# Seven-product pairs of a hybrid decoder step: sums formed in PSUM banks, and equal halves in the mixer

## The chip, the cores and the metric

The kernel runs on one core of one Trainium2 chip. The core has TensorE (PE; PEld is its loading of weights), VectorE (DVE), ScalarE (ACT), GpSimd (POOL) and SyncE (SP), which issues most DMAs. TensorE writes its products to PSUM, which has eight banks of 512 numbers for each of 128 partitions; the kernel holds four of them under the tag "acc" and four under the tag "ps". The metric is the device time of one execution in microseconds (us); lower is better.

## The reference

One inference step of one decoder layer, for 512 prompt tokens with 16 meta tokens ahead of them, and for 8 sequences of 4 new tokens: in all 560 columns of tokens, of which 544 (the meta tokens left out) go on after attention. The model has width 1024 and 2816 hidden units.

```python
def swiglu(x, w_gate, w_up, w_down):
    return (jax.nn.silu(x @ w_gate) * (x @ w_up)) @ w_down

h = x + 0.5 * rms_norm(swiglu(rms_norm(x, ffn1_pre_g), ...), ffn1_post_g)
u = rms_norm(h, mix_pre_g)
proj = u @ w_in      # q, k, v, rank and r of the GLA branch; q, k, v of attention; gate_a, gate_b
...
o_a = rms_norm(o_a, gla_norm_g) * jax.nn.silu(r_a)
m = jax.nn.sigmoid(gate_a) * (o_a @ w_o_gla) + jax.nn.sigmoid(gate_b) * (o_b @ w_o_sb)
h = h + rms_norm(m @ w_out, mix_post_g)
y = h + 0.5 * rms_norm(swiglu(rms_norm(h, ffn2_pre_g), ...), ffn2_post_g)
```

All values are float32.

## The kernel before

Activations are held turned: 128 features in the partitions, tokens along the columns. Each operand of a large product is split in two parts, a high part hi (a cast to the type fp32r) and a low part lo (what is left), and a product of two is three matmuls: hi with hi, hi with lo, lo with hi. A weight block is loaded by DMA into one of three buffers "raw"; ScalarE casts it into one of three buffers "hi", VectorE subtracts into one of three buffers "lo". Buffers of a name are used in turn.

The stages are: first feed-forward part (gate and up products, then the down product), w_in products with GLA and attention, the mixer (gates r, a and b, and the products o and p with w_o_gla and w_o_sb), the product with w_out, the second feed-forward part. The order on TensorE, VectorE, ScalarE and GpSimd is written out by hand: a product is a generator that yields after every few matmuls, each yield is one step, and `later(n, f)` and `when(n, f)` put a piece of work in the n-th step from now or from the start of a stage. Within a step work stands in the order in which it was asked for, and work of `later` ahead of work of `when`.

**Pairs of seven products.** Where two blocks of weights and two halves of the tokens meet, four quarter products are formed from seven instead of eight (a scheme of Strassen and Winograd). This is done for 16 pairs in each of the two feed-forward parts (`seven`, L1221, gate and up of one tile f), for 10 pairs in the mixer (`seven_steps`, L1016, through `r_pair`, L2320, and `gate_pair`, L2352), and for the down products (`pair`, L1371, which the change leaves as it is). A pair has 84 matmuls in 14 steps of six. They come in seven phases of 12, each with one bank as its target; the table at L1262 and L1042 lists bank, activation, weights and their quarter:

- a gets its first product; d the product of s1; b that of s2; c that of s3;
- a gets a second product and is then the result c11; d gets s4; c gets the product with t4.

The weights of a pair are cast as four groups: b1 (used by a and d), t (by b and c), b2 (by a and d), t4 (by c). `weights_at` (L1008) puts the cast of b1 six steps ahead of the pair, so in step 8 of the pair before, that of t two steps ahead, b2 with the start, and t4 in step 4. ScalarE copies the first products of a and d to SBUF (e1, e5), and five additions on VectorE do the rest: u2 = e1 + b, v = e5 + c, c22 = u2 + v, c12 = u2 + d, c21 = u2 + c. All pairs use the four banks "acc".

**Room.** SBUF tiles of the names "room" lie in an arena whose places come from a table (`PLACES`, L52).

**Plain products** in the mixer (`tile_steps`, L691) take the 544 columns as halves of 280 (`HW`) and 264 (`W1`); pairs take them as halves of 272 (`QW`). In the first feed-forward part a half has 280 columns, in the second 272.

Of the kernel before, what the change touches and what calls it, by code (L numbers as in the profile page):

```python
# [18 lines left out]
KD = D // P  # L19
# [33 lines left out]
0c060018121e242a7094908082848668766a5066565e5c787c5452724e7a5836221c884c8c6c3064484a6e60613a2e8a3e446236923c465a3036  # L53
281674404260917e91588e124e328c341e726c307e4a4c188a486e3e24647a882c3c38360c06625a6a42749244402a3a2e0c00605e5c1e201254
147c16220664465283006268826980660b50560660680a69866467808400620b660a0c2661066460676686186300606266671004650662646766
86286100646066671a10620660878663660c1c00621d8786640e2506662486871c60910064688786241a690666688687820a6800246564697662
6806666991008264690078680607082491770776681c069186424e3e343a74546e7266323c00368c4468767c2840781e6c820c0238708c762a2e
26927c8a040660622a2c4816246527702e1262186071152c622a2b2d6415712c1262632a622a2b2d642c71626306180c1e62714b71246a003254
883e64604b38020434308a6058763c786222122a482e4c4a8e2c7b84668c687e7f406056464f3d333579036b366e747044426c7215015939318b
7782893f055514157a804e5a7e825c2483284e655e92647c508d3a521e148c822667648466616764656766422c7016604668746c6e647244206a  # L60
0a6612088a6c1804343c8c780688916a761a720f026e22320e1c103057565584641486544000760c676a6c8a7248082e604c1a3e582a910e2c66
301c856e001257421002685655542040164675150c8a146a0a300e121e188c782a2c007074107620060421863442736c6e728988846475668e0c
17343e12324c4a42460b7476486a3c1c3004436e20080972621a3736876660860a436c8417686e8e6a642c1488568c430408063c906394708417
6664606c6e78728e8a68846a86606e17708468646a6c7894728e668a0c866e606c176478686a848e728a66706e6c866072177084026836646a6c
8e00786686948a6e401c6620721a1e178a646030948e106c0c6a0e181c2068708486366e786a4072102a221e20170094667038840e1a6e8e0c1c
60724068641c8a1e1a186c220260206e8e59540e2a0c84721e302e68100066606c94641e3840202200706694308e8464606e4740721002682e0e
6c6630002a6884548c880c1456648e6e701660946c586e0c040e463c144754621206329074442e087674582c0a6c160c40102e2c006611466e43
705658544472340862403010322a1200024406343090916e0a436d0610160c72620840909066466c726c625670540a58406e084672020e540a6e
44163c4000100c064614404372561213020410703c3d423e000e4c6e161246483c060444420b1048704c0a023e494072006e480e14166e424412
463c560a2a7460309461704c8c8d2e904a4862766660346c6d670e88303276406c8c6663629500102c623e8876947254586667000e0a01006667  # L70
00105466403e88560d0c7273000c068a508e86202264366a1e7c7880268492524e34603a141a7e487a68734246824a733c3e58901b1717722e38
6e174c2840245a17175c7074442a5e5d1876668c54509212583e903c12151556622c88526c1b484a464215687f7b7e7a151b683a4e601b6a845c
1b18678d8053932d3078156577556381891c2282516d57648a5e1272384c2e1e828e906e868418403e36582416749432426a340c00605a5c484a
30683c44463a0c4e62702a56882c121e922022066416547f00607a7e7b80660b768c0662640a650c6c677e7800640e66060a600f06620e67660c
7a1000641166670e0419066218676610801800641966671a0c1906621c181d660a1b0064241a251c18630666266227241a65001c286429261067
06244e664f280e5000261d1c064e62520624292800501c4f00264e080928062524020308006c14862c486672504c8e4e1268926052880208047a
64304a2e3c82600a5884220c0280566a622410460e1e360842000a060418200302060e10030211060c0d0504020c110304020e1005030c181e30
24363d3440243a3e243865268202906c626e70
# [56 lines left out]
def hybrid_step(  # L135
# [555 lines left out]
    def tile_steps(act, w1, order=range(KD)):  # L691

        wid = (HW, w1)
        hi, lo = st.parts.pop(0)
        acc = {h: ps("acc") for h in range(2)}
        for k in order:
            a = {h: act.get(k, h, wid[h]) for h in range(2)}
            for h in range(2):
                T.matmul(acc[h][:, : wid[h]], hi[k], a[h][0], start=(k == order[0]), stop=False)  # L699
                T.matmul(acc[h][:, : wid[h]], hi[k], a[h][1], start=False, stop=False)  # L700
# [315 lines left out]
    def seven_steps(f, act, qw, outs):  # L1016
# [6 lines left out]
        def add(name, x, y):  # L1023
            o[name] = take(HW)
            tt(o[name][:, :qw], o[x][:, :qw], y[:, :qw], ALU.add)
            give(o.pop(x))

# [4 lines left out]
        def made(name, x, y, last=None):  # L1032
            tt(outs[name], o[x][:, :qw], y, ALU.add)
            if last:
                give(o.pop(last))
# [58 lines left out]
    def other_tiles(old, gain, rs, nw, wid, hid, pairs, plan, late, sums_at, begun):  # L1094
# [126 lines left out]
        def seven(f):  # L1221
            a11, a12, a22 = ([ub.t[k0 + k, h] for k in range(4)] for h, k0 in ((0, 0), (0, 4), (1, 4)))
            s1, s2, s3, s4 = ([sums[j, k] for k in range(4)] for j in range(4))
            a, d, b, c = (ps("acc") for _ in range(4))
            o = {}

            def add(name, x, y):
                o[name] = take(HW)
                tt(o[name][:, :QW], o[x][:, :QW], y[:, :QW], ALU.add)
# [5 lines left out]
            def u2_():  # L1235
                add("u2", "e1", b)
                give(o["e1"])

            def v_():
                add("v", "e5", c)  # L1240
                give(o["e5"])

            def c22():
                o["up"], o["sl"] = take(NT), take(NT)
                tt(o["up"][:, QS[1]], o["u2"][:, :QW], o["v"][:, :QW], ALU.add)
                give(o["v"])

            def c21():
                tt(o["sl"][:, QS[1]], o["u2"][:, :QW], c[:, :QW], ALU.add)
                give(o["u2"])  # L1250
# [11 lines left out]
            for x, act, key, k0, first in ((a, a11, "b1", 0, True), (d, s1, "b1", 4, True), (b, s2, "t", 0, True), (c, s3, "t", 4, True),  # L1262
                                           (a, a12, "b2", 4, False), (d, s4, "b2", 0, False), (c, a22, "t4", 0, False)):
# [8 lines left out]
        waiting = []  # L1272
# [1001 lines left out]
    def split(dst, k, src, kept):  # L2274
# [3 lines left out]
        for h in range(2):  # L2278
            c = slice(h * HW, h * HW + W2[h])
# [19 lines left out]
    def gate_r(n):  # L2299

        o = oa_back(n)
        acc = yield from tile_steps(um, W1)
        sg = take(NW)

        def sig():
            for h in range(2):
                S.activation(sg[:, h * HW : h * HW + W2[h]], acc[h][:, : W2[h]], AF.Sigmoid)

        def by():
            for h in range(2):  # L2310
                c = slice(h * HW, h * HW + W2[h])
                tt(sg[:, c], acc[h][:, : W2[h]], sg[:, c], ALU.mult)
# [7 lines left out]
    def r_pair(n):  # L2320
# [12 lines left out]
        def first():  # L2333
            t[0] = take(NW)
            outs.update(c11=lambda a: S.copy(t[0][:, q0], a), c21=t[0][:, q1])
# [16 lines left out]
    def gate_pair(what, n):  # L2352
# [3 lines left out]
        outs = {"c11": lambda a: S.activation(t0[:, q0], a, AF.Sigmoid), "c12": t1[:, q0], "c22": t1[:, q1], "c21": t0[:, q1]}  # L2356
        later(15, lambda: S.activation(t1, t1, AF.Sigmoid))
        later(16, lambda: S.activation(t0[:, q1], t0[:, q1], AF.Sigmoid))
# [38 lines left out]
    def out_a(n):  # L2397
        acc = yield from tile_steps(oas, W1, (0, 1, 2, 7, 3, 4, 6, 5) if n == 0 else range(KD))
        m1.append(take(NW))

        def out():
            for h in range(2):
                S.copy(m1[n][:, h * HW : h * HW + W2[h]], acc[h][:, : W2[h]])
# [28 lines left out]
    with tc.manual_schedule(engines={E.PE, E.DVE, E.Activation, E.Pool}):  # L2432
# [31 lines left out]
        def product_b(n):  # L2464
            acc = yield from tile_steps(obs, W1)
            mixed(n, acc)

        def chain():
            mains = {"r": gate_r, "o": out_a, "p": product_b}
            for kind, what, t in MIXER:  # L2470
# [3 lines left out]
                if (what, t) == ("b", 6):  # L2474
                    later(1, lambda: give(*kept_sums, *(t for p in um.full.values() for t in p)))

# [107 lines left out]
        def mixed(n, acc):  # L2584
            t = sgb[n]

            def by():
                for h in range(2):
                    c = slice(h * HW, h * HW + W2[h])
# [160 lines left out]
```

## Time and profile before

| | |
|---|---|
| time, median of 3 runs | 1492.96 us (1492.42 to 1494.59) |
| profiled execution | span 1491.2 us from its first to its last instruction; its time with what lies around it is not listed |
| granted clock of TensorE | 0.999 of full speed |
| pairs, first part | 93.4 to 266 us |
| pairs, mixer | 832 to 1044 us |
| pairs, second part | 1179.5 to 1348 us |
| DMA | 182 MB, 122 GB/s on average |

The matmuls of a pair stand at L1266 to L1268 and L1046 to L1048, plain products of the mixer at L699, L700 and L702. The additions on VectorE are written through a helper, so all of them stand at L166 and are told apart by their tiles. A row of groups gives line, engine, operation, output and inputs, shape and count, then busy time, the mean of one in ns, and the idle time of the engine just before them with what ended it. Matmuls overlap: one lasts 290 ns from its start to its end, and the next starts some 128 ns after it.

### The profile page before, as it was taken

Reading aid. Unit: us, or ns where it says so; the run is one execution under the profiler, and the core shown is the slowest. Engines: PE = TensorE matmul, PEld = TensorE weight load, DVE = VectorE, ACT = ScalarE, POOL = GpSimd, SP = SyncE. Lnnn points to the kernel's source line nnn. Section 1 sums busy time; section 2 is a strip of 40 time slices with the busy share of each in tenths; the row PEclk is TensorE's granted clock in tenths of the full one; section 3 lists DMA queues with packets and bytes.
Section 4 is the critical chain, followed back from the end, with each engine's and each line's share of the span. In section 5 each row is a group of like instructions: output and inputs, shape, how many; then the busy total and the mean of one; then the engine's idle time right before and its main releaser. Section 6 shows DMA issues by size and latency. Waiting matters only on the chain.

```text
span 1491.2 us, 29865 instructions
## 1 busy us (share of the span) xinstructions
PE 1482.6 (99%) x11909; PEld 1435.2 (96%) x11909; DVE 1106.0 (74%) x1945; ACT 783.1 (53%) x1453; POOL 68.4 (5%) x145
## 2 busy tenths in 40 slices
PE   9999999999999999999999999999999999999998
PEld 8999999999999899999998999999999999999998
DVE  5888888855677866877887845777567898888544
ACT  7455454533555656566666543634564455455333
POOL 2000000000000011112111000000000000000000
PEclk9999999999999999999999999999999999999999
DMA  8133333324665584336555866344531333333253
GB/s 253 50 92 100 100 96 92 97 79 123 172 153 138 148 151 100 86 95 161 125 112 160 228 162 200 96 110 140 155 111 52 100 100 100 99 107 92 79 152 115
DMA packets 277230, 181.97 MB, mean 122 GB/s; under 512 B 10429, under 2 KB 255363, under 8 KB 277091
## 3 DMA queue, kind: packets, MB, share of 16 engines
q1 hardware_dynamic: 276786, 180.00, 44.7%
q8 instruction: 93, 1.52, 0.4%
q14 instruction: 47, 0.38, 0.1%
q0 software_dynamic: 288, 0.07, 0.0%
q10 hardware_dynamic: 16, 0.00, 0.0%
HBM read 155.06 MB, written 24.97 MB: 121 GB/s over the span
## 4 chain that ended last, share of the span: by engine, by line
PE 96%; DVE 2%; ACT 1%; DMA 1%; issue 0%; DVEq 0%; ACTq 0%
PE acc L1266 8%; PE acc L1267 8%; PE acc L1268 8%; PE acc L699 7%; PE acc L700 7%; PE acc L702 7%; PE acc L712 6%; PE acc L715 6%; PE acc L713 6%; PE acc L1046 2%; PE acc L1047 2%; PE acc L1048 2%; PE acc L1209 2%; PE acc L1206 2%; PE acc L1207 2%; PE ps L2041 1%
## 5 line engine op out<-in xcount | busy, mean ns | idle before, releaser
L166 DVE TENSOR_TENSOR room<-room,room 128x544 f32<-128x544 f32 (+18 forms) x457 | 285.6, 648 | 72.3 <-ACT room L779 16.7
L166 DVE TENSOR_TENSOR lo<-raw,hi 128x1024 fp32r<-128x1024 f32 (+1 forms) x207 | 248.1, 1199 | 105.5 <-ACT hi L678 66.7
L1266 PE MATMUL acc<-room,hi 128*128 128x280 f32 (+1 forms) x896 | 260.0, 290 | 0.0
L1268 PE MATMUL acc<-room,lo 128*128 128x280 f32 (+1 forms) x896 | 259.6, 290 | 0.0
L1267 PE MATMUL acc<-room,hi 128*128 128x280 f32 (+1 forms) x896 | 259.4, 289 | 0.0
L699 PE MATMUL acc<-room,hi 128*128 128x280 f32 x832 | 241.1, 307 | 0.2 <-DVE room L169 0.2
L700 PE MATMUL acc<-room,hi 128*128 128x280 f32 x832 | 225.0, 289 | 0.0
L977 ACT CAST hi<-raw 128x1024 fp32r<-128x1024 f32 x100 | 104.8, 1052 | 146.2 <-PE acc L1267 48.6
L702 PE MATMUL acc<-room,lo 128*128 128x280 f32 x832 | 173.1, 289 | 0.0
L1267 PEld LDWEIGHTS acc<-room,hi 128*128 128x128 f32 x896 | 168.9, 188 | 0.0
L1266 PEld LDWEIGHTS acc<-room,hi 128*128 128x128 f32 x896 | 168.8, 188 | 0.0
L1268 PEld LDWEIGHTS acc<-room,lo 128*128 128x128 f32 x896 | 168.6, 188 | 0.0
L699 PEld LDWEIGHTS acc<-room,hi 128*128 128x128 f32 x832 | 156.8, 188 | 10.1 <-issue 8.1
L700 PEld LDWEIGHTS acc<-room,hi 128*128 128x128 f32 x832 | 157.2, 189 | 1.2
L678 ACT CAST hi<-raw 128x1024 fp32r<-128x1024 f32 (+1 forms) x107 | 108.2, 1013 | 75.2 <-issue 21.5
L702 PEld LDWEIGHTS acc<-room,lo 128*128 128x128 f32 x832 | 130.3, 189 | 0.0
L977 ACT CAST hi<-room 128x1024 fp32r<-128x1024 f32 x92 | 76.9, 836 | 87.3 <-PE acc L1267 58.5
L166 DVE TENSOR_TENSOR lo<-room,hi 128x1024 fp32r<-128x1024 f32 x92 | 87.9, 955 | 43.4 <-ACT hi L977 43.0
L712 PE MATMUL acc<-room,hi 128*128 128x280 f32 (+2 forms) x388 | 110.8, 295 | 0.0
L713 PE MATMUL acc<-room,hi 128*128 128x280 f32 (+2 forms) x388 | 108.9, 290 | 0.0
L166 DVE TENSOR_TENSOR room<-room,acc 128x272 f32<-128x272 f32 (+1 forms) x180 | 76.2, 437 | 43.8 <-PE acc L1048 20.9
L712 PE MATMUL acc<-room,room 128*128 128x280 f32 (+3 forms) x364 | 107.4, 295 | 0.0
(397 smaller groups left out, 3437.2 us busy)
## 6 DMA issues: line engine op xcount, KB each, us to landing
raw<-in_w_in_dram SPq DMA_DIRECT2D x43, 512.0 KB, 7.2
raw<-in_ffn_w_gate_dram SPq DMA_DIRECT2D x64, 256.0 KB, 3.1
raw<-in_ffn_w_up_dram SPq DMA_DIRECT2D x64, 256.0 KB, 3.4
raw<-in_ffn_w_down_dram SPq DMA_DIRECT2D x36, 448.0 KB, 3.9
raw<-in_w_in_dram SPq DMA_DIRECT2D x40, 256.0 KB, 4.7
out_dram<-room SPq DMA_DIRECT2D x36, 256.0 KB, 3.7
room<-in_cache_k_dram SPq DMA_DIRECT2D x32, 256.0 KB, 5.7
room<-in_cache_v_dram SPq DMA_DIRECT2D x32, 256.0 KB, 4.7
```

The source lines that it names most:

```text
L166: (eng or V).tensor_tensor(out=out, in0=a, in1=b, op=op)
L678: S.copy(h_, src)
L699: T.matmul(acc[h][:, : wid[h]], hi[k], a[h][0], start=(k == order[0]), stop=False)
L700: T.matmul(acc[h][:, : wid[h]], hi[k], a[h][1], start=False, stop=False)
L702: T.matmul(acc[h][:, : wid[h]], lo[k], a[h][0], start=False, stop=(k == order[-1]))
L712: T.matmul(acc[h][:nw, : wid[h]], wh, a[h][0], start=(k == 0), stop=False)
L713: T.matmul(acc[h][:nw, : wid[h]], wh, a[h][1], start=False, stop=False)
L715: T.matmul(acc[h][:nw, : wid[h]], wl, a[h][0], start=False, stop=(k == kt - 1))
L977: S.copy(hi[:, :kt], src)
L1266: T.matmul(x[:, :QW], hi, act[k][0], start=(first and k == 0), stop=False, skip_group_check=True)
L1267: T.matmul(x[:, :QW], hi, act[k][1], start=False, stop=False, skip_group_check=True)
L1268: T.matmul(x[:, :QW], lo, act[k][0], start=False, stop=(k == 3), skip_group_check=True)
```

## The change

The pairs of `seven` and `seven_steps` keep their seven products and change how these are added. Bank b no longer starts from zero: ScalarE copies the finished first product of a into bank b, and b's matmuls add to it, so that b ends as u2. Then ScalarE copies b into bank c, and c's first product adds to that (u3 = u2 + product of s3); after the second product of c the bank holds c21. VectorE is left with c22 = u3 + e5 and c12 = u2 + d, and ScalarE copies e5, u2 and u3 to SBUF. The second product of a moves ahead of the first of c. c21 goes straight from bank c through ScalarE's function (Silu, Sigmoid, or a copy).

In `seven` the pairs use the banks "acc" and "ps" in turn; ahead of the second pair of each part, which is the first on "ps", one matmul each is written to b and c with start set. In the mixer the halves of plain products become 272 and 272. `PLACES` has new numbers for the changed order of tiles.

```diff
-    def tile_steps(act, w1, order=range(KD)):
-        wid = (HW, w1)
+    def tile_steps(act, w1, order=range(KD), w0=HW):
+        wid = (w0, w1)
...
         # seven_steps (mixer)
-        for n, g in ((3, lambda: copied("e1", a)), (5, lambda: copied("e5", d)), (7, lambda: add("u2", "e1", b)),
-                     (9, lambda: add("v", "e5", c)), (10, lambda: made("c22", "u2", o["v"][:, :qw], "v")),
-                     (11, lambda: outs["c11"](a[:, :qw])), (13, lambda: made("c12", "u2", d[:, :qw])),
-                     (15, lambda: made("c21", "u2", c[:, :qw], "u2"))):
+        def seeded(x, y):
+            S.copy(x[:, :qw], y[:, :qw])
+        for n, g in ((2, lambda: seeded(b, a)), (4, lambda: copied("e5", d)), (6, lambda: seeded(c, b)), (6, lambda: copied("u2", b)),
+                     (10, lambda: copied("u3", c)), (11, lambda: outs["c11"](a[:, :qw])), (11, c22),
+                     (12, lambda: made("c12", "u2", d)), (14, lambda: outs["c21"](c[:, :qw]))):
             later(n, g)
-        for x, act_, key, k0, first in ((a, a11, "b1", 0, True), (d, s1, "b1", 4, True), (b, s2, "t", 0, True), (c, s3, "t", 4, True),
-                                        (a, a12, "b2", 4, False), (d, s4, "b2", 0, False), (c, a22, "t4", 0, False)):
+        for x, act_, key, k0, first in ((a, a11, "b1", 0, True), (d, s1, "b1", 4, True), (b, s2, "t", 0, False), (a, a12, "b2", 4, False),
+                                        (c, s3, "t", 4, False), (d, s4, "b2", 0, False), (c, a22, "t4", 0, False)):
...
         # seven (feed-forward parts); its table of phases changes in the same way
-            a, d, b, c = (ps("acc") for _ in range(4))
+            tag = turns[len(turns_done) % 2]
+            turns_done.append(f)
+            a, d, b, c = (ps(tag) for _ in range(4))
-            for n, g in ((3, lambda: copied("e1", a)), (5, lambda: copied("e5", d)), (7, u2_), (9, v_), (10, c22),
-                         (11, lambda: S.activation(o["sl"][:, QS[0]], a[:, :QW], AF.Silu)),
-                         (13, lambda: tt(o["up"][:, QS[0]], o["u2"][:, :QW], d[:, :QW], ALU.add)), (15, c21),
-                         (16, lambda: S.activation(o["sl"][:, QS[1]], o["sl"][:, QS[1]], AF.Silu)), (18, all_)):
+            for n, g in ((2, lambda: seeded(b, a)), (4, lambda: copied("e5", d)), (6, lambda: seeded(c, b)), (6, lambda: copied("u2", b)),
+                         (8, c11), (10, lambda: copied("u3", c)), (11, c22), (12, c12),
+                         (14, lambda: S.activation(o["sl"][:, QS[1]], c[:, :QW], AF.Silu)), (16, all_)):
                 later(n, g)
+            if len(turns_done) == 2:
+                for x in (b, c):
+                    T.matmul(x[:, :QW], quarters[f, "b1"][0][:, 0], a11[0][0], start=True, stop=True, skip_group_check=True)
...
         # gate_r; out_a, product_b, split and mixed change in the same way
-        acc = yield from tile_steps(um, W1)
+        acc = yield from tile_steps(umq, QW, w0=QW)
```

Two places of the order show what moves. The first is ScalarE in one pair of the first feed-forward part. Before, with banks acc133 (a), acc134 (d), acc135 (b) and acc136 (c); hi132 is b2 of this pair, hi138 its t4, hi139 is b1 of the next pair and hi141 its t:

```order
L977 CAST hi132_1912<-raw120_1748 128x1024 [waits DMAHW0_49,DMAHW7_49,DVE_49,PE_49]
L1260 ACTIVATE room36_7_72<-room36_7_72 128x280 [waits DVE_49]
L1233 COPY room96_51_1019<-acc133_1915 128x280 [waits PE_49]
L977 CAST hi138_1951<-room98_50_886 128x512 [waits PE_49,Activation_49]
L1233 COPY room96_51_1019<-acc134_1916 128x280 [waits PE_49]
L977 CAST hi139_1985<-raw127_1803 128x1024 [waits DVE_49,DMAHW1_49,PE_49,Activation_49]
L1258 ACTIVATE room12_1_66<-acc133_1915 128x280 [waits PE_49]
L977 CAST hi141_2019<-room0_3_68 128x1024 [waits DVE_49,PE_49,Activation_49]
```

The same stretch of ScalarE in the changed kernel, with the same names of banks and casts (L1233 copies a bank into a bank, L1230 a bank to SBUF):

```order
L976 CAST hi132_1916<-raw120_1751 128x1024 [waits DMAHW7_49,DMAHW0_49,DVE_49]
L1233 COPY acc135_1921<-acc133_1919 128x280 [waits PE_49]
L1230 COPY room6_51_746<-acc134_1920 128x280 [waits PE_49]
L976 CAST hi138_1954<-room124_57_1199 128x512 [waits DVE_49]
L1233 COPY acc136_1922<-acc135_1921 128x280 [waits PE_49]
L1230 COPY room78_9_89<-acc135_1921 128x280
L1237 ACTIVATE room24_6_71<-acc133_1919 128x280 [waits PE_49]
L976 CAST hi139_1989<-raw127_1806 128x1024 [waits DVE_49,DMAHW1_49,PE_49,Activation_49]
L1230 COPY room42_49_696<-acc136_1922 128x280 [waits PE_49]
L976 CAST hi141_2023<-room54_55_1006 128x1024 [waits DVE_49,PE_49,Activation_49]
```

The copy of acc136, the bank c, now stands right behind the cast of hi139. The buffer of hi139 is the one that t of this pair had (three casts earlier among the hi buffers), so that the cast waits for the last matmul with t: this was in the fourth phase and is now in the fifth.

The second place is TensorE at the start of the pair's seventh phase, the second product of c with t4 (hi138). Before:

```order
L1266 MATMUL acc134_1916<-room18_53_1050,hi132_1912 128x280
L1267 MATMUL acc134_1916<-room30_52_1048,hi132_1912 128x280
L1268 MATMUL acc134_1916<-room18_53_1050,lo132_1913 128x280
L1266 MATMUL acc136_1918<-room114_25_171,hi138_1951 128x280 [waits DVE_49]
L1267 MATMUL acc136_1918<-room108_31_248,hi138_1951 128x280
L1268 MATMUL acc136_1918<-room114_25_171,lo138_1952 128x280
```

And in the changed kernel, at the same phase:

```order
L1265 MATMUL acc134_1920<-room60_56_1068,hi132_1916 128x280
L1266 MATMUL acc134_1920<-room60_56_1068,hi132_1916 128x280
L1267 MATMUL acc134_1920<-room60_56_1068,lo132_1917 128x280
L1265 MATMUL acc136_1922<-room0_46_597,hi138_1954 128x280 [waits Activation_49]
L1266 MATMUL acc136_1922<-room72_47_609,hi138_1954 128x280
L1267 MATMUL acc136_1922<-room0_46_597,lo138_1955 128x280 [waits DVE_49]
```

The first matmul that writes to c again waited for VectorE, which read c for v; it now waits for ScalarE, which copies c as u3. The cast of hi138 stands further ahead on ScalarE than that copy.

More of the change, by code (lines that the diff above doesn't have):

```diff
@@ L57 @@
[L57 to L61, printed above, removed]
@@ L79 @@
+36704486648c0e486e24663a74507e90101276881e4c0640944a3e0004808a68841802782a74242e3c00502c7e54784e4f0251504f7e742a4e7f
+53754e040375747f027e5352181e244e12581554560278041352124302487e1674946a
 """)
@@ L1021, in seven_steps @@
         o = {}
[L1023 to L1026, printed above, removed]
         def copied(name, x):
@@ L1233, in copied, with seeded, c11, c12 @@
                 S.copy(o[name][:, :QW], x[:, :QW])
[L1235 to L1241, printed above, removed]
-            def c22():
[L1244 to L1249, printed above, removed]
+            def seeded(x, y):
+                S.copy(x[:, :QW], y[:, :QW])
+            def c11():
+                o["sl"] = take(NT)
+                S.activation(o["sl"][:, QS[0]], a[:, :QW], AF.Silu)
+            def c22():
+                o["up"] = take(NT)
+                tt(o["up"][:, QS[1]], o["u3"][:, :QW], o["e5"][:, :QW], ALU.add)
+                give(o["u3"], o["e5"])
+            def c12():
+                tt(o["up"][:, QS[0]], o["u2"][:, :QW], d[:, :QW], ALU.add)
                 give(o["u2"])
@@ L1270, in seven @@
                         yield
-        waiting = []
+        waiting, turns, turns_done = [], ("acc", "ps"), []
         def hidden_or_wait(f, sl, at):
@@ L2278, in split @@
         for h in range(2):
-            c = slice(h * HW, h * HW + W2[h])
+            c = slice(h * QW, h * QW + QW)
             dst.t[k, h] = (hi[:, c], lo[:, c])
@@ L2306, in sig @@
             for h in range(2):
-                S.activation(sg[:, h * HW : h * HW + W2[h]], acc[h][:, : W2[h]], AF.Sigmoid)
+                S.activation(sg[:, h * QW : h * QW + QW], acc[h][:, :QW], AF.Sigmoid)
         def by():
             for h in range(2):
-                c = slice(h * HW, h * HW + W2[h])
-                tt(sg[:, c], acc[h][:, : W2[h]], sg[:, c], ALU.mult)
+                c = slice(h * QW, h * QW + QW)
+                tt(sg[:, c], acc[h][:, :QW], sg[:, c], ALU.mult)
             tt(o, o, sg, ALU.mult)
@@ L2334, in first @@
             t[0] = take(NW)
-            outs.update(c11=lambda a: S.copy(t[0][:, q0], a), c21=t[0][:, q1])
+            outs.update(c11=lambda a: S.copy(t[0][:, q0], a), c21=lambda c: S.copy(t[0][:, q1], c))
         def by_t(i):
@@ L2355, in gate_pair @@
         q0, q1 = slice(0, QW), slice(QW, NW)
-        outs = {"c11": lambda a: S.activation(t0[:, q0], a, AF.Sigmoid), "c12": t1[:, q0], "c22": t1[:, q1], "c21": t0[:, q1]}
+        outs = {"c11": lambda a: S.activation(t0[:, q0], a, AF.Sigmoid), "c12": t1[:, q0], "c22": t1[:, q1],
+                "c21": lambda c: S.activation(t0[:, q1], c, AF.Sigmoid)}
         later(15, lambda: S.activation(t1, t1, AF.Sigmoid))
-        later(16, lambda: S.activation(t0[:, q1], t0[:, q1], AF.Sigmoid))
         if what == "b":
@@ L2397, in out_a @@
     def out_a(n):
-        acc = yield from tile_steps(oas, W1, (0, 1, 2, 7, 3, 4, 6, 5) if n == 0 else range(KD))
+        acc = yield from tile_steps(oas, QW, (0, 1, 2, 7, 3, 4, 6, 5) if n == 0 else range(KD), QW)
         m1.append(take(NW))
@@ L2402, in out @@
             for h in range(2):
-                S.copy(m1[n][:, h * HW : h * HW + W2[h]], acc[h][:, : W2[h]])
+                S.copy(m1[n][:, h * QW : h * QW + QW], acc[h][:, :QW])
         later(1, out)
@@ L2464, in product_b @@
         def product_b(n):
-            acc = yield from tile_steps(obs, W1)
+            acc = yield from tile_steps(obs, QW, w0=QW)
             mixed(n, acc)
@@ L2475, in chain @@
                     later(1, lambda: give(*kept_sums, *(t for p in um.full.values() for t in p)))
+        umq = Parts()
+        for k in range(KD):
+            for h in range(2):
+                umq.t[k, h] = tuple(t[:, h * QW : h * QW + QW] for t in um.full[k])
         mixer = chain()
@@ L2588, in by @@
                 for h in range(2):
-                    c = slice(h * HW, h * HW + W2[h])
-                    tt(t[:, c], acc[h][:, : W2[h]], t[:, c], ALU.mult)
+                    c = slice(h * QW, h * QW + QW)
+                    tt(t[:, c], acc[h][:, :QW], t[:, c], ALU.mult)
             def hi():
```

61 lines of the change are left out of this document (31 added, 30 removed).

## The prediction

> **What bounds the kernel now.** I read the page's first part, then the waits of TensorE, then stretches of equal work side by side, then single instructions in order of time.
>
> ```profile
> span 1491.2 us, 29865 instructions
> ## 1 busy us (share of the span) xinstructions
> PE 1482.6 (99%) x11909; PEld 1435.2 (96%) x11909; DVE 1106.0 (74%) x1945; ACT 783.1 (53%) x1453; POOL 68.4 (5%) x145
> ```
> TensorE (PE) is busy for 99% of the span, VectorE (DVE) for 74%, ScalarE (ACT) for 53%. The change takes work from VectorE and gives about as much to ScalarE. That pays only where TensorE waits for VectorE, so that is the next view: who TensorE waited for, in total us, times, longest.
>
> ```profile
> PE acc L1493 <- DVE own L270: 1.1, 1, 1.1
> PE acc L715 <- DVE lo L166: 0.6, 1, 0.6
> ...
> PE ps L873 <- DVE room L166: 0.2, 1, 0.2
> ```
> These are the first two and the last of its eight rows; the eight add up to 3.5 us, and none of them is at a line of the seven-product pairs (L1046 to L1048, L1266 to L1268). There is nothing to win from shorter VectorE queues in the pairs. The next rows are three stretches: one pair of the first feed-forward part, one of the second, and a stretch of the last down product.
>
> ```profile
> 201.50:212.30 10.80, 10.80 (x86) 10.80 (x85) 9.31 (x15) 5.31 (x8) 0.00 (x0) 1.00 0.33 96
> 1274.20:1284.80 10.60, 10.60 (x87) 10.60 (x87) 9.32 (x15) 5.24 (x8) 0.00 (x0) 1.00 0.36 104
> 1395.00:1405.00 10.00, 10.00 (x82) 10.00 (x81) 2.45 (x2) 2.48 (x3) 0.00 (x0) 1.00 0.17 48
> ```
> The columns are length, PE, weight loads, DVE, ACT, POOL, granted clock (1.00), DMA share. The last two hold matmuls of the same shape (272 columns): 87 in 10.60 us with VectorE busy for 9.32, and 82 in 10.00 us with VectorE busy for 2.45. With 0.29 us for the matmul that sticks out at an end, that is 125.2 and 125.5 ns each. So the spacing does not depend on what VectorE and ScalarE do. A pair lasts 84 spacings, whatever its additions cost.
>
> **What the change does to the path.** *Equal halves.* A half of 280 columns and one of 264 become two of 272.
>
> ```profile
> L700 PE MATMUL acc<-room,hi 128*128 128x280 f32 x576 | 162.5, 291 | 0.0
> L700 PE MATMUL acc<-room,hi 128*128 128x264 f32 x256 | 73.0, 285 | 0.0
> L1266 PE MATMUL acc<-room,hi 128*128 128x272 f32 x448 | 129.1, 288 | 0.0
> ```
> One matmul of each takes 291, 285 and 288 ns, and 291 + 285 = 2 x 288: nothing.
>
> *Fewer additions.* In the two feed-forward parts 32 pairs, and in the mixer 10, lose three VectorE additions each, 42 x 3 = 126, and gain three to four ScalarE copies each.
>
> ```profile
> L166 DVE TENSOR_TENSOR room<-room,acc 128x272 f32<-128x272 f32 x110 | 46.4, 434 | 32.1 <-PE acc L1048 20.9 <-PE acc L1268 8.6 <-PE acc L1432 1.3
> L1233 ACT COPY room<-acc 128x280 f32<-128x280 f32 x32 | 12.5, 390 | 0.8
> ```
> That is 126 x 0.43 = 54 us less on VectorE and, at 0.39 us each, about 50 us more on ScalarE. Both run beside TensorE, and both have room: 9.3 and 5.3 of 10.8 us. I cost this at nothing by itself.
>
> *Two matmuls before each feed-forward part's second pair*, four in all, at 0.128 us: +0.5 us.
>
> *The new waits.* TensorE now waits for ScalarE at three places of each pair: before bank b, before the first half of c, and before the second half of c. For each I compare when ScalarE can be done with when TensorE arrives. These are instructions of one pair of the first part in order of time (start, duration):
>
> ```profile
> 201.51 0.29 PE L1266 MATMUL acc<-room,hi 128*128 128x280 f32 x1
> 204.46 0.69 DVE L166 TENSOR_TENSOR room<-raw,raw 128x512 f32<-128x512 f32 x1
> 204.71 0.62 ACT L977 CAST hi<-room 128x512 fp32r<-128x512 f32 x1 [1.07 <-PE acc L1267]
> 205.24 0.39 ACT L1233 COPY room<-acc 128x280 f32<-128x280 f32 x1
> 207.68 0.30 PE L1266 MATMUL acc<-room,hi 128*128 128x280 f32 x1
> 207.80 1.06 ACT L977 CAST hi<-raw 128x1024 fp32r<-128x1024 f32 x1 [2.17 <-DVE room L166]
> ```
> The pair starts at 201.51 and its fifth phase at 207.68: 48 spacings of 128.5 ns, 1.54 us for each of the seven phases of 12 matmuls. The cast at 207.80 starts 0.12 us after the phase that last read its buffer. The copy at 205.24 starts 0.09 us before the cast ahead of it ends (204.71 + 0.62): ScalarE overlaps instructions that have nothing left to wait for.
>
> The seeds of b and c have a whole phase, 1.54 us, between the end of what they copy and the matmuls that need it: 0.12 us until they start, and 0.39 us each. A copy from one bank to another is not in this trace; the nearest row is that copy out of a bank (0.39), and the farthest that I would allow is the cast of 1024 columns (1.06). Either fits into the phase, so I take 0.39 and no wait. Less than nothing it cannot be, since TensorE does not wait there now.
>
> The third place is the tight one. u3 is the copy of c between its two halves. It stands on ScalarE right behind the cast of the next pair's first weights (hi139 in the rows of the change), and this cast has moved: its buffer is read last by c's first half, which was the fourth phase and is now the fifth. So cast and copy have to fit into the one phase between the halves of c. Counted from the end of the fifth phase: 0.12 until the cast starts, 1.06 for it, less 0.09 of overlap, 0.39 for the copy: done at 1.48 us. What a late release costs is seen where TensorE waits for the down weights:
>
> ```profile
> 375.67 0.94 ACT L678 CAST hi<-raw 128x896 fp32r<-128x896 f32 x1 [4.80 <-DMA raw<-in_ffn_w_down_dram]
> 376.65 1.09 DVE L166 TENSOR_TENSOR lo<-raw,hi 128x896 fp32r<-128x896 f32 x1 [4.51 <-ACT hi L678]
> 376.67 0.19 PEld L712 LDWEIGHTS acc<-room,hi 128*128 128x128 f32 x1
> ...
> 376.90 0.29 PE L713 MATMUL acc<-room,hi 128*128 128x280 f32 x1
> ...
> 377.79 0.19 PEld L715 LDWEIGHTS acc<-room,lo 128*128 128x128 f32 x1 [0.83 <-DVE lo L166]
> ...
> 378.02 0.29 PE L712 MATMUL acc<-room,hi 128*128 128x280 f32 x1
> ```
> The weight load starts 0.05 to 0.06 us after its releaser ends (376.61 to 376.67, 377.74 to 377.79). It was due when the matmul before it began, at 376.90, so it was 0.89 us late; the next matmul but one started at 378.02 in place of 376.90 + 2 x 0.128 = 377.16, 0.86 us late. So lost time is lateness less 0.03. In the new pair the load of the seventh phase is due 11 spacings after the fifth phase's end, at 1.41 us, and released at 1.48 + 0.05 = 1.53: 0.12 late, **0.09 us lost**. For the second part's width:
>
> ```profile
> 1274.26 0.28 PE L1266 MATMUL acc<-room,hi 128*128 128x272 f32 x1
> 1280.30 0.29 PE L1266 MATMUL acc<-room,hi 128*128 128x272 f32 x1
> 1280.41 1.05 ACT L977 CAST hi<-raw 128x1024 fp32r<-128x1024 f32 x1 [2.10 <-PE acc L1267]
> ```
> Here the cast starts 0.11 us behind the phase, done at 0.11 + 1.05 - 0.09 + 0.38 = 1.45, released at 1.50, and 11 spacings of 125.5 ns are 1.38: 0.12 late, 0.09 lost again. Queued behind the waiting matmul is only TensorE's own stream, so each loss lengthens the span. The mixer's pairs have the same cast, or one of equal size for a plain product, right ahead of u3. In one of them (the pair r 3) another copy stands between:
>
> ```profile
> L2130 ACT COPY room<-ps 128x512 f32<-128x512 f32 x32 | 19.2, 600 | 10.1 <-PE ps L2128 9.3 <-ACT room L2130 0.6
> ```
> less 0.09 of overlap, 0.5 us more there, if nothing else of TensorE's work stands in that phase.
>
> *Moved with the cast.* VectorE's subtraction that makes the low part lo starts when the cast ends, and the DMA that refills the raw buffer goes out when lo is done:
>
> ```profile
> L166 DVE TENSOR_TENSOR lo<-raw,hi 128x1024 fp32r<-128x1024 f32 x171 | 209.1, 1223 | 86.4 <-ACT hi L678 47.7 <-ACT hi L977 38.1
> raw<-in_ffn_w_gate_dram SPq DMA_DIRECT2D x64, 256.0 KB, 3.1
> ```
> Both come one phase, 1.54 us, later. Counted in the pair, lo is done at 7.70 + 0.12 + 1.06 + 1.22 = 10.1, and the next pair needs it at its third matmul, 10.8 + 0.26. With 3.1 us to landing the refill is there at 13.3, and VectorE first reads it 3 us into the next pair (204.46 against 201.51), at 13.8. Both are covered; without that cover they would cost what they are late by.
>
> **The sum.** 42 x 0.09 = 3.8, + 0.5 for r 3, + 0.5 for the added matmuls = 4.8 us. In the mixer the first four pairs stand among TensorE work of the attention, which can fill the gap, so I take 4.5. The profiled span becomes 1495.7. It lies 1.8 us under the median of the three runs (1492.96), so the time becomes **1497.5 us**.
>
> **Rivals.** (1) *u3 is in time.* The cast waits for the last but one matmul of the phase; were it 0.1 us earlier than the two rows say, the loss is gone: 1492.96 + 0.5 = 1493.5. For it: 0.09 us is the difference of five terms. Against: both widths give it. (2) *The wait is longer.* If u3 does not overlap with the cast, 0.09 us more for each pair, 1497.5 + 3.8 = 1501.3; and the first plain product after a mixer pair has its weights' lo on VectorE behind the addition of c12, which now comes in the twelfth step, up to 0.3 us for five of them: 1502.8. (3) *Faster: matmuls in the pairs move closer*, because VectorE reads and writes PSUM less. TensorE has 42 x 84 = 3528 spacings there; from 1.0 ns of each it would make up for the 0.5 us and gain 3 us, and with 2 ns it is 1493.5 - 7.1 = 1486.4. Against it stand 125.2 and 125.5 ns with VectorE nearly full and nearly idle. The Trainium skill, "TensorE: Matmul & The Clock Gate", "Back-to-back issue gap", gives N/2.4 + 2.5 ns for a lone stream, an estimate of 115.8 ns for 272 columns, so that something in this kernel would take 9.5 ns from every matmul; by that rule, if VectorE were the cause, 33 us could be had. The trace does not agree with the cause: the spacing is as long where VectorE idles. (4) *The change does not remove the waits it is aimed at*: that is so already, as the waits of TensorE show none in the pairs, and is part of the forecast.
>
> **How the numbers follow.** Forecast 0.47, (1) 0.28, (2) 0.20, (3) 0.05. A measurement of this kernel can tell about 0.2%, 3 us, from no change: faster is under 1490.0, slower is over 1495.9. Rival (1) and a tenth of the forecast (some pairs late, some not) are the same; the rest of the forecast and (2) are slower: 0.05, 0.33, 0.62. The range goes from rival (1) less 1 us for the scatter of runs, 1492.5, to the end of (2), 1503.
>
> **What would show it.** In the changed profile TensorE's waits should have a row for the matmuls of L1265 and L1045 on ScalarE's copy of c, near 0.1 us each, one for each pair, and no row for the seeds. The seventh phase should start about 0.09 us late and the other phases keep 128.5 and 125.5 ns. The forecast is wrong if the u3 copy ends under 1.36 us after the fifth phase, or if a wait shows at the seeds (a bank to bank copy over 1.3 us), or if the spacing itself moves.

## The result, and the profile after

The changed kernel takes **1500.42 us** (median of 4 runs, 1500.21 to 1501.21), the kernel before 1492.89 us beside it: a ratio of 1.0049, 95% interval 1.0035 to 1.0063. It is 7.5 us slower; 4.5 were forecast, in a range of 1492.5 to 1503.0.

The first part of the page of the changed kernel (engine, busy us, share, instructions):

```profile
span 1498.5 us, 29770 instructions
PE 1487.7 (99%) x11913; PEld 1438.4 (96%) x11913; DVE 1056.4 (70%) x1819; ACT 817.7 (55%) x1581; POOL 68.5 (5%) x145
```

VectorE has 126 instructions and 50 us less, ScalarE 128 instructions and 35 us more, TensorE the four added matmuls. The forecast had 54 us less for VectorE and about 50 more for ScalarE. The span grew by 7.3 us, so nothing is seen of a gain from the relief of VectorE, and something else was paid. TensorE's waits (line, whom it waited for, total us, times, longest), the first five:

```profile
PE acc L1492 <- DVE own L269: 1.1, 1, 1.1
PE acc L1045 <- ACT room L2402: 0.9, 1, 0.9
PE acc L714 <- DVE lo L165: 0.7, 1, 0.7
PE acc L711 <- ACT hi L677: 0.7, 1, 0.7
PE acc L1045 <- DVE room L165: 0.6, 1, 0.6
```

The first and the third were there before. The second, the fourth and the fifth are new, and the second and the fifth stand at a line of the mixer's pairs. Each is one long wait, not the small one per pair that was forecast. The small one has no row in this view; it shows only where one matmul's start is compared with the next. I laid the starts of the same matmuls of both traces beside each other and took the difference at the ends of stretches:

| stretch (times of before) | lost there, us |
|---|---|
| 0 to 92.5: ahead of the first pair | 0.77 |
| 92.5 to 266.5: 16 pairs of the first part | 1.38 |
| 266.5 to 380: rest of the first part, start of the down product | 1.25 |
| 380 to 831: down, w_in, GLA, attention | -0.10 |
| 831 to 1046: mixer, 10 pairs | 3.09 |
| 1046 to 1178 | -0.10 |
| 1178 to 1349: 16 pairs of the second part | 1.29 |
| 1349 to the end | 0.06 |

*The pairs of the first part.* One pair of the changed kernel in order of time (start, duration), rows of ScalarE, TensorE and its weight loads:

```profile
210.96 0.29 PE L1265 MATMUL acc<-room,hi 128*128 128x280 f32 x1
211.07 1.05 ACT L976 CAST hi<-raw 128x1024 fp32r<-128x1024 f32 x1 [1.06 <-PE acc L1266]
212.03 0.39 ACT L1230 COPY room<-acc 128x280 f32<-128x280 f32 x1
212.37 0.29 PE L1267 MATMUL acc<-room,lo 128*128 128x280 f32 x1
212.46 0.19 PEld L1265 LDWEIGHTS acc<-room,hi 128*128 128x128 f32 x1
212.50 0.36 PE L1265 MATMUL acc<-room,hi 128*128 128x280 f32 x1
212.69 0.29 PE L1266 MATMUL acc<-room,hi 128*128 128x280 f32 x1
```

The fifth phase ends at 210.96. The cast of the next b1 starts 0.11 us later, the copy u3 follows 0.09 us before its end and is done at 212.42. The weight load of the seventh phase was due when the matmul ahead of it began, at 212.37, and starts at 212.46, 0.09 us late. The first matmul lasts 0.36 in place of 0.29, and the next starts 0.19 us after it in place of 0.13: 0.07 us lost. This is the forecast's chain with each member within 0.03 us. In the first part 13 of 16 pairs show 0.07 us, in the second part 13 of 16 show 0.09, and nine of the mixer's ten 0.06 to 0.11; the rest have less. It adds up to 2.9 us. The seeds cost nothing in the feed-forward parts; in one pair of the mixer (at 960.2 us) the seed of b stands behind another operation of ScalarE and 0.07 us is lost. The copies from bank to bank are as short as those out of a bank:

```profile
L1027 ACT COPY acc<-acc 128x272 f32<-128x272 f32 x20 | 7.5, 375 | 9.5 <-PE acc L1047 9.5
```

And the same stretches of equal work as before (length, PE, weight loads, DVE, ACT, POOL, clock, DMA share):

```profile
204.20:215.00 10.80, 10.80 (x85) 10.77 (x84) 8.06 (x12) 6.03 (x12) 0.00 (x0) 1.00 0.33 96
1271.80:1282.40 10.60, 10.60 (x86) 10.55 (x85) 8.12 (x12) 6.07 (x12) 0.00 (x0) 1.00 0.34 98
```

VectorE's 9.31 and 9.32 us became 8.06 and 8.12. As many matmuls fit into the stretch as before, less the one that the delay costs: the spacing did not move.

*The stop at the down product.* The chain of waits lists its longest pieces. Two loads stand among the five longest of the changed kernel (start, length, what):

```profile
367.49 8.14 DMA raw<-in_ffn_w_down_dram
971.61 8.57 DMA raw<-in_w_in_dram
```

Before, the second was not among them, and in place of the first stood a load issued after it. The issues on SP's queue around the first, and the cast that waited for it, in the changed kernel:

```profile
364.81 0.37 SPq L650 DMA_DIRECT2D room<-in_w_in_dram  x1
365.23 0.97 SPq L1311 DMA_DIRECT2D room<-h_dram  x2
367.49 0.38 SPq L198 DMA_DIRECT2D raw<-in_ffn_w_down_dram  x1
...
375.73 1.04 ACT L677 CAST hi<-raw 128x1024 fp32r<-128x1024 f32 x1 [5.11 <-DMA raw<-in_ffn_w_down_dram]
```

and of the kernel before:

```profile
365.20 0.38 SPq L199 DMA_DIRECT2D raw<-in_ffn_w_down_dram  x1
365.63 0.58 SPq L651 DMA_DIRECT2D room<-in_w_in_dram  x1
...
369.82 1.05 ACT L678 CAST hi<-raw 128x1024 fp32r<-128x1024 f32 x1 [1.43 <-DMA raw<-in_ffn_w_down_dram]
```

The early load of a block of w_in (512 KB) now goes out ahead of the down weights, not behind them, and they reach ScalarE 8.2 us after their issue in place of 4.6. No line of the change names this load. Its room has another place now, and in the new program the load waits on a semaphore of TensorE, where it waited for nothing before. Against the profile of before the stop costs 1.1 us. That profile has a wait of its own here, 0.6 us at L715 in the prediction's rows, and none of the three other traces of the code before (runs 7 and 8) has it; against those the stop costs 1.7 to 1.9 us.

*Two pairs of the mixer.* The pair that starts at 896.5 us loses 1.0 us at the start of its second phase:

```profile
898.62 0.67 ACT L2402 COPY room<-acc 128x272 f32<-128x272 f32 x2
899.05 0.19 PEld L1045 LDWEIGHTS acc<-room,hi 128*128 128x128 f32 x1 [1.08 <-ACT room L2402]
```

Its second phase writes bank d, and waits for a copy out of the plain product before it. The explanation that run 3 tests: banks are handed out in turn, in the order in which the tiles are first written. Before, that was a, d, b, c; now b is first written by ScalarE's seed, ahead of d's first matmul, so the turn is a, b, d, c, and d gets the bank of the product that has just ended. The pair at 982.8 us loses 0.65 us in its first and 0.87 us in its second phase:

```profile
969.20 0.45 DVE L165 TENSOR_TENSOR room<-room,room 128x272 f32<-128x272 f32 x1 [2.99 <-ACT room L1024]
969.56 0.43 DVE L165 TENSOR_TENSOR room<-room,acc 128x272 f32<-128x272 f32 x1
969.91 1.22 DVE L165 TENSOR_TENSOR lo<-raw,hi 128x1024 fp32r<-128x1024 f32 x1
971.19 0.92 SPq L637 DMA_DIRECT2D raw<-in_w_in_dram  x2
980.28 0.69 DVE L165 TENSOR_TENSOR room<-raw,room 128x512 f32<-128x512 f32 x1 [1.61 <-DMA raw<-in_w_in_dram]
983.62 0.19 PEld L1047 LDWEIGHTS acc<-room,lo 128*128 128x128 f32 x1 [0.60 <-DVE lo L165]
985.74 0.19 PEld L1045 LDWEIGHTS acc<-room,hi 128*128 128x128 f32 x1 [0.82 <-DVE room L165]
```

c22 (969.20) waits for u3, c12 and then lo stand behind it, and the refill of lo's raw buffer goes out at 971.19, 11.0 us after its pair began (960.2). Before it was 8.4 us (963.94 against 955.5). Its second half (971.61 in the chain above) lands 8.57 us later, and the subtraction at 980.28 waits for it with all of VectorE's later work behind.

### The profile page after: what moved, and what is told of

The parts are those of the page before. It is cut to its first block, busy times and chain, and to the rows that moved or that the text cites. A ratio compares the mean times of both kernels' runs of the same rounds, so it can differ in the third digit from the quotient of the medians.

```text
span 1498.5 us, 29770 instructions
## 1 busy us (share of the span) xinstructions
PE 1487.7 (99%) x11913; PEld 1438.4 (96%) x11913; DVE 1056.4 (70%) x1819; ACT 817.7 (55%) x1581; POOL 68.5 (5%) x145
## 3 DMA queue, kind: packets, MB, share of 16 engines
q8 instruction: 93, 1.52, 0.4%
## 4 chain that ended last, share of the span: by engine, by line
PE 94%; DVE 2%; DMA 2%; ACT 1%; issue 0%; DVEq 0%; SPq 0%; ACTq 0%
PE acc L698 7%; PE acc L711 6%; PE acc L714 6%; PE acc L712 6%; PE acc L699 6%; PE acc L701 6%; PE acc L1265 4%; PE ps L1265 4%; PE acc L1267 4%; PE ps L1267 4%; PE acc L1266 4%; PE ps L1266 4%; PE acc L1045 2%; PE acc L1046 2%; PE acc L1047 2%; PE acc L1208 2%
## 5 line engine op out<-in xcount | busy, mean ns | idle before, releaser
L165 DVE TENSOR_TENSOR room<-room,room 128x544 f32<-128x544 f32 (+13 forms) x464 | 287.2, 641 | 86.7 <-ACT room L1024 16.6
L698 PE MATMUL acc<-room,hi 128*128 128x280 f32 (+1 forms) x832 | 240.3, 306 | 0.2 <-DVE room L168 0.2
L699 PE MATMUL acc<-room,hi 128*128 128x280 f32 (+1 forms) x832 | 225.3, 289 | 0.0
L701 PE MATMUL acc<-room,lo 128*128 128x280 f32 (+1 forms) x832 | 172.9, 289 | 0.0
L698 PEld LDWEIGHTS acc<-room,hi 128*128 128x128 f32 x832 | 156.7, 188 | 10.1 <-issue 8.1
L699 PEld LDWEIGHTS acc<-room,hi 128*128 128x128 f32 x832 | 157.1, 189 | 1.2
L1265 PE MATMUL acc<-room,hi 128*128 128x280 f32 (+1 forms) x448 | 130.9, 292 | 0.0
L1265 PE MATMUL ps<-room,hi 128*128 128x280 f32 (+1 forms) x448 | 130.9, 292 | 0.0
L701 PEld LDWEIGHTS acc<-room,lo 128*128 128x128 f32 x832 | 130.6, 188 | 0.0
L1267 PE MATMUL acc<-room,lo 128*128 128x280 f32 (+1 forms) x448 | 129.7, 290 | 0.0
L1267 PE MATMUL ps<-room,lo 128*128 128x280 f32 (+1 forms) x448 | 129.7, 290 | 0.0
L1266 PE MATMUL acc<-room,hi 128*128 128x280 f32 (+1 forms) x448 | 129.6, 289 | 0.0
L1266 PE MATMUL ps<-room,hi 128*128 128x280 f32 (+1 forms) x448 | 129.5, 289 | 0.0
L711 PE MATMUL acc<-room,room 128*128 128x280 f32 (+3 forms) x359 | 105.8, 295 | 0.0
L712 PE MATMUL acc<-room,room 128*128 128x280 f32 (+3 forms) x365 | 105.7, 290 | 0.0
L714 PE MATMUL acc<-room,room 128*128 128x280 f32 (+3 forms) x361 | 104.5, 289 | 0.0
```

The lines of the kernel that those rows point to most:

```text
L165: (eng or V).tensor_tensor(out=out, in0=a, in1=b, op=op)
L711: T.matmul(acc[h][:nw, : wid[h]], wh, a[h][0], start=(k == 0), stop=False)
L712: T.matmul(acc[h][:nw, : wid[h]], wh, a[h][1], start=False, stop=False)
L714: T.matmul(acc[h][:nw, : wid[h]], wl, a[h][0], start=False, stop=(k == kt - 1))
L1265: T.matmul(x[:, :QW], hi, act[k][0], start=(first and k == 0), stop=False, skip_group_check=True)
L1266: T.matmul(x[:, :QW], hi, act[k][1], start=False, stop=False, skip_group_check=True)
```

## The experiments

Each ran beside the kernel before; times are medians, ratios are to the kernel before with their 95% interval. The kernel before took 1492.89 us beside the changed kernel and 1493.18 to 1493.35 us beside the experiments, so a difference from the changed kernel is uncertain by some 0.5 us. A change under 0.2% cannot be told from none by time alone; the place where a wait was or was not is read from the trace.

**1. c22 straight from the bank.**

```diff
-  (10, lambda: copied("u3", c)), (11, c22)      # c22 = u3 + e5
+  (10, c22)                                     # c22 = bank c + e5, on VectorE
-  for key, d, e in (("b1", -6, -5), ...
+  for key, d, e in (("b1", -6, -4), ...
```

> The changed kernel, but c22 is added on VectorE straight from bank c, so the copy u3 on ScalarE is gone, and the subtraction that makes lo of b1 stands one step later so that c22 is ahead of it. In the changed profile the second step of the seventh phase is 0.07 us late in 13 of 16 pairs of the first part, 0.09 us in the second part, and 0.04 to 0.10 us in the mixer, 2.9 us in all. Theory (u3 is late because it stands behind the cast of b1 on ScalarE): VectorE is done 0.12 + 0.45 = 0.57 us after the fifth phase, due is 1.41, so the delay at the seventh phase goes and the time falls by 2.9 us, 1500.4 to 1497.5. Rival (it is the turn of a bank between an engine that reads it and TensorE that adds to it, whichever engine reads): the delay stays at 0.07 to 0.09 us, 1500.4.

1497.86 us, 1.0030 (1.0019 to 1.0041): 2.6 us less than the changed kernel. VectorE now stands where ScalarE's copy stood:

```profile
210.43 1.05 ACT L976 CAST hi<-raw 128x1024 fp32r<-128x1024 f32 x1 [1.06 <-PE acc L1267]
210.52 0.45 DVE L165 TENSOR_TENSOR room<-acc,room 128x280 f32<-128x280 f32 x1 [1.23 <-PE acc L1268]
211.60 0.28 PE L1267 MATMUL acc<-room,hi 128*128 128x280 f32 x1
211.72 0.29 PE L1268 MATMUL acc<-room,lo 128*128 128x280 f32 x1
211.86 0.29 PE L1266 MATMUL acc<-room,hi 128*128 128x280 f32 x1
211.98 0.29 PE L1267 MATMUL acc<-room,hi 128*128 128x280 f32 x1
```

It is done at 210.97, and the seventh phase (211.86) runs on at 0.12 us behind a step of 0.14. The delay at the seventh phase is gone in every pair that had one. The rival, a fixed cost of the bank's turn, falls: the bank is read and added to as before, by another engine.

**2. u3 copied twice.**

```diff
-  (10, lambda: copied("u3", c)),
+  (10, lambda: copied("u3", c)), (10, lambda: S.copy(o["u3"][:, :QW], c[:, :QW])),
```

> The changed kernel, but the copy u3 is made twice, one right behind the other. Theory (TensorE waits at the seventh phase for ScalarE's queue: cast, copy): each of 42 pairs loses 0.39 - 0.09 = 0.30 us more, 12.6 us in all, 1513.0 (1511 to 1514). Rival (the 0.07 to 0.09 us come from a fixed turn of the bank and ScalarE has room there): under 2 us more, 1500.4 to 1502.4.

1519.29 us, 1.0174 (1.0159 to 1.0190): 18.9 us more than the changed kernel, beyond both. TensorE's waits and ScalarE's rows show why it is more than 12.6:

```profile
PE ps L1265 <- ACT room L1254: 4.2, 16, 0.5
PE acc L1265 <- ACT room L1254: 3.7, 16, 0.2
PE acc L1045 <- ACT room L1038: 2.1, 9, 0.3
```

```profile
216.49 0.39 ACT L1230 COPY room<-acc 128x280 f32<-128x280 f32 x1
216.91 0.39 ACT L1254 COPY room<-acc 128x280 f32<-128x280 f32 x1
```

The second copy starts 0.03 us after the end of the first and does not overlap with it, probably because it writes the same tile: 0.42 us per pair, not 0.30. The wait is now long enough to be listed, 41 times, and in 41 pairs that is 17.2 us; two pairs of the first part lose 0.3 us more each. The queue theory holds; the expectation counted on an overlap that did not take place.

**3. Bank d ahead of bank b, in the whole mixer.**

```diff
-  for n, g in ((2, lambda: seeded(b, a)), ...
+  for n, g in ((3, lambda: seeded(b, a)), ...   # seven_steps only
```

> The changed kernel, but in the mixer the copy of a into b is asked for one step later, so that bank d is handed out ahead of bank b. In the changed kernel the pair at 896.5 us waits 1.02 us at the start of its second phase, whose target is d, for the copies of the plain product before it (L2402). Theory (b, now written first by ScalarE, takes the bank that was d's, and d gets the bank of the product just ended): that wait goes, the time falls by 0.8 to 1.1 us to 1499.5. Rival (ScalarE is late there whatever bank it is): the wait turns up at the third phase with the same length, 1500.4.

1505.57 us, 1.0083 (1.0068 to 1.0099): 5.2 us more, a miss. The pair at 896.5 us did lose its wait (1.02 us to none), so the bank theory holds there. But the seed now stands behind other work of ScalarE, and in four pairs the third phase waits for it, as the rival has it, though not in the pair that it named:

```profile
PE acc L1045 <- ACT acc L1027: 4.4, 4, 2.2
```

**4. The w_in block behind the down weights.** One column of its room is written by ScalarE first, so that the load waits for it.

```diff
+  def go():
+      S.copy(room[:, :1], ones[:, :1])
       nc.sync.dma_start(room..., win[...])
+  later(1, go)
```

> The changed kernel, but the early load of a block of w_in (512 KB, L650) goes out behind the loads of the down weights at 371.9 us and not ahead of them at 364.8. In the changed profile the load of the down weights that was issued at 367.5 reached ScalarE 8.2 us later, in the profile of before 4.6 us, and TensorE stood 1.3 us longer there. Theory (the loads share the queue, and the new places of the tiles let the w_in block go first): the 1.3 us go, 1499.1. Rival (that stop has another reason, such as the later refills): it stays, 1500.4.

1498.84 us, 1.0036 (1.0022 to 1.0049). The cast that waited 5.11 us has this row:

```profile
373.26 1.05 ACT L682 CAST hi<-raw 128x1024 fp32r<-128x1024 f32 x1 [1.46 <-DMA raw<-in_ffn_w_down_dram]
...
379.79 0.37 SPq L653 DMA_DIRECT2D room<-in_w_in_dram  x1
```

TensorE waits nowhere from 373 to 378.5 us, and the same matmuls gain 1.96 us there on the changed kernel. That is more than the 1.1 us which the stop costs against the profile of before, since there TensorE waited at this place too (0.86 us, in the prediction's rows). The block's load goes out at 379.79 us, later than intended and later than in the kernel before (365.63 us), so this run takes the load away from the down weights and does not restore the old order. The time fell by 1.6 us. In this profile the first 19 us, long before the edit, were 1.2 us longer than in that of the changed kernel, so the time is a poorer witness here than the place. It is shown that the stop goes with this load. That the new places caused the new order is not shown: no run changed the places alone.

**5. All together, with c12 behind lo in the mixer.**

```diff
+  (the edits of 1, 3 and 4)
-  (12, lambda: made("c12", "u2", d)),
+  (13, lambda: made("c12", "u2", d)),
```

> The three edits together, and in the mixer the addition of c12 one step later, so that it stands behind the subtraction that makes lo, and the load that refills that buffer goes out about 1 us sooner. Theory (the four causes are apart): 1500.4 less 2.9 (copy u3), 1.1 (bank d), 1.3 (load order) and 1.0 (of the 1.4 us that the pair at 983 us waits for a refill that was 2.5 us late) is 1494.1, no faster than before by more than 0.2%. Rival (the edits hide one another's gain or bring new waits): 1496 to 1500.

1499.01 us, 1.0037 (1.0023 to 1.0051): the rival's outcome, and by the edit of 3 once more (`PE acc L1051 <- ACT acc L1032` with 4.2 us in 4 waits). So one thing was taken back.

**6. The same, with the late seed in one pair only.**

```diff
-  ((3, lambda: seeded(b, a)), ...
+  ((2 + (f == ("a", 0)), lambda: seeded(b, a)), ...
```

> As the run with the edits together, but the copy of a into b is later only in the one pair at 896.5 us that waited for bank d; in all other pairs it is where the change puts it. Theory (the late copies made the waits of 1.0, 2.3, 0.9 and 0.9 us at the third phase of four other pairs, and nothing else is open): 1500.4 less 2.6 (copy u3, as measured), 1.8 (load of the down weights), 1.1 (bank d) and 1.4 (refill) is 1493.5, within 0.2% of before. Rival (waits only move on to the next place): 1496 or more.

**1493.76 us**, 1.0001 (0.9992 to 1.0010): within 0.3 us of the sum, and no longer to be told from the kernel before. TensorE's waits are those of before, without the 0.6 us at the down product (which other traces of the code before do not have either) and with one of 0.3 us at a pair (L1051), what is left of the late refill. That now goes out 10.0 us after the pair began (965.50 against 955.5), and the pair at 978 us loses 0.54 us where it lost 1.52, and 1.65 with the edit of 1 alone. The edit that acts at this place is VectorE's order, so c12 ahead of lo was worth 1.1 us there. The kernel is not faster than the one before: nothing that the change takes away was on the path.

**7. More additions in the kernel before**, each one a repetition that writes the same values to the same tile.

```diff
-  tt(o[name][:, :QW], o[x][:, :QW], y[:, :QW], ALU.add)
+  for _ in range(2): tt(...)       # u2, v, c22: twice each; in the second run three times each
```

> The kernel before, but three of the five additions of each pair (u2, v, c22) are made twice, 126 additions and 54 us more on VectorE, as many as the change takes away. Theory (VectorE's queue is beside the path in the pairs, so what the change takes from it brings nothing): within 0.2% of before, 1493. Rival (VectorE, at 9.3 of 10.8 us per pair, is close to the bound, and its additions cost time): with 1.3 us more it is at 10.6 of 10.8, low parts and refills come late, 5 us or more, over 1498.

> The kernel before, with u2, v and c22 of each pair made three times: six additions more per pair. With three more, VectorE was busy for 10.47 of 10.80 us of a pair of the first part (9.31 before, so 0.39 us each) and no time was lost. Theory (VectorE is beside the path until its work per pair is longer than TensorE's): six make 11.6 us in the first part and 11.5 of 10.60 in the second, so each of some 30 pairs there becomes 0.8 to 1.0 us longer, 24 to 30 us in all, and the mixer's ten some more: 1517 to 1530. Rival (TensorE is the bound whatever VectorE does): 1493.

Three more: 1493.63 us, 1.0001 (0.9992 to 1.0010). Six more: 1533.90 us, 1.0273 (1.0256 to 1.0290). The first of the two stretches of before, with three more:

```profile
201.50:212.30 10.80, 10.80 (x86) 10.80 (x85) 10.47 (x18) 5.30 (x9) 0.00 (x0) 1.00 0.33 97
```

and with six more, 60 us of the first part, then the longest row of TensorE's waits:

```profile
200.00:260.00 60.00, 55.42 (x421) 54.28 (x421) 58.63 (x101) 25.44 (x40) 0.00 (x0) 1.00 0.31 88
```

```profile
PE acc L1270 <- DVE room L166: 30.7, 28, 1.7
```

VectorE could take 1.16 us more in a pair of 10.8 at almost no cost: in the trace two pairs of the second part lose 0.3 and 0.1 us, and no other pair loses any. At 58.63 of 60 it is the bound, and TensorE waits at 28 pairs. The time lies above the expected 1517 to 1530: most pairs of the feed-forward parts became 1.2 to 1.4 us longer, not 0.8 to 1.0, and the expectation had counted VectorE's busy time and not the gaps between its instructions. So the kernel before had slack at VectorE for three additions more, and three fewer only add to it.

**8. Equal halves alone, in the kernel before.**

```diff
-  acc = yield from tile_steps(um, W1)
+  acc = yield from tile_steps(umq, QW, w0=QW)     # and so in out_a, product_b and what reads them
```

> The kernel before with one part of the change alone: the plain products of the mixer in halves of 272 and 272, not 280 and 264. Theory (spacing is linear in the columns): within 0.1% of before, 1493. Rival (the halves are what costs time in the mixer): 1495 or more.

1492.60 us, 0.9995 (0.9986 to 1.0004): nothing that the time can tell, as forecast; in the trace the mixer is 0.4 us shorter.

## Why the prediction was right, and what it left out

- *Nothing to win* held: without the 126 additions and with what the change broke put back, the time is that of before (run 6), and 126 additions more cost next to nothing (run 7).
- *Equal halves: nothing* held (run 8). *Four added matmuls: 0.5 us* held: the shift between the two traces grows by 0.25 us at each of the two places.
- *u3 is late by 0.12, 0.09 us lost* held in its mechanism (runs 1 and 2). Its size: 0.07 us in the first part, 0.09 in the second, 0.06 to 0.11 in the mixer, and less in a few pairs. The sum of 3.8 + 0.5 us measured 2.9 by the trace and 2.6 by the time of run 1, since the first part lost less per pair, and because the 0.5 us for the pair r 3 did not come: that pair lost 0.09 us there; it lasts 15.2 us, not 10.5, with attention work of TensorE between its phases. Of the first four mixer pairs one (at 851.2 us) lost nothing. Taking 4.5 for 4.8 was the right direction, and too little.
- *The wait has a row* failed as a sign: 0.07 us is not listed in the waits of TensorE. The starts of successive matmuls show it.
- *Both are covered* is the step that failed. It took 3.1 us from issue to landing, the median of the first part's loads, for all pairs. In the mixer one half of a refill took 8.57 us to land and had no cover, and lo stood behind c12: 1.5 us at one pair, of which 1.1 went with the order of run 6. (In its working, 10.1 + 3.1 is 13.2, not 13.3; the cover in the first part is the better for it.)
- Two terms were missing from the sum: a seed that takes its bank ahead of d (1.1 us), and a load that new places move ahead of another (1.1 us at the stop). With them 2.6 + 0.5 + 1.5 + 1.1 + 1.1 = 6.8 us, where the last term is against the one profile of before. The 0.8 us ahead of the first pair are left. The other traces of the changed code reached it between 0.3 us sooner and 1.2 us later than this one, and those of the code before 0.1 to 0.6 us later than the profile of before, so I take most of the 0.8 us for scatter.
- The forecast's own causes, u3 and the added matmuls, make 3.1 of the 7.5 us. Another 3.7 us come from three places for which it had no term, or one of nothing. That 1500.4 still fell inside the range is luck: the range's upper end came from rival (2), which did not happen.
- Of the rivals, (3), closer matmuls, fell: 10.8 us hold the same 84 spacings with VectorE busy for 8.06, 9.31 or 10.47 us. With it falls the estimate from the Trainium skill, "TensorE: Matmul & The Clock Gate", "Back-to-back issue gap", as a reason to hope for time here: that figure is for a lone stream, as the prediction says, and here each matmul has a weight load of its own (x11909 of both in the page). The time went towards the end of (2), but not by (2): copy and cast do overlap, and no plain product waited for its lo.

## What to carry to other kernels

Before taking work from an engine, repeat some of that work and see whether the time moves: if more costs nothing, less brings nothing. When an operation moves to another engine, list besides its duration which queue it stands in and behind what, which bank or buffer it claims and in which turn, and which loads go out after it. A median time to landing is no cover for a stage whose loads are slower than the median.

## What the hardware showed

In run 3 TensorE stood still for 2.2 us in one pair, and what followed cost 1.6 us more. Rows of TensorE, and three stretches with the granted clock (the figure ahead of the DMA share), one ahead of the wait, one behind it, and one later:

```profile
988.69 0.39 PE L1045 MATMUL acc<-room,hi 128*128 128x272 f32 x1 [2.17 <-ACT acc L1027]
...
989.59 0.43 PE L1047 MATMUL acc<-room,lo 128*128 128x272 f32 x1
989.82 0.43 PE L1045 MATMUL acc<-room,hi 128*128 128x272 f32 x1
```

```profile
984.00:986.00 2.00, 2.00 (x19) 2.00 (x18) 2.00 (x5) 0.88 (x1) 0.00 (x0) 1.00 0.59 174
989.20:992.60 3.40, 3.40 (x18) 3.40 (x17) 0.69 (x1) 0.94 (x3) 0.00 (x0) 0.50 0.42 124
994.00:997.00 3.00, 3.00 (x25) 2.95 (x25) 0.69 (x2) 1.63 (x3) 0.00 (x0) 1.00 0.00 0
```

From 989.2 to 992.6 us the matmuls start 0.23 us apart in place of 0.125, and the clock is 0.50: a wait of 2.2 us cost 4.0. In run 5 the clock was also 0.50 for as long, behind a wait of 2.0 us. Waits of up to 1.7 us (the run with six more additions) had no such tail. The Trainium skill, "TensorE: Matmul & The Clock Gate", "Part 1: The HAM clock gate (the "warmup" mystery)", has the clock halved after an idle window of some 3.4 us; here 2.2 us were enough, and the slow stretch of 3.4 us agrees with the length that it gives for the return.
